# Where a matmul's two operands stand in a 128-byte row: weights of every sixth unit placed instead of one activation chunk, and modulation products emitted one unit later

## The chip, the cores and the metric

The kernel runs on one core of one Trainium2 chip. The metric is the device time of one launch in microseconds (us). Before the change the median of three runs is 2653.69 us (2653.15 to 2655.44).

## The reference

The reference is a two-layer encoder trunk on 256 tokens of 2048 features, all in float32. Cut to what matters:

```python
for l in range(DEPTH):                                   # 2 layers
    mod = silu(c) @ ada_w[l] + ada_b[l]                  # 6 * 2048 values
    sh_a, sc_a, gt_a, sh_m, sc_m, gt_m = split(mod, 6)
    h = rmsnorm(x, norm_mix[l]) * (1 + sc_a) + sh_a
    qa, ka, va, qb, kb, vb, ga, gb = split_cols(h @ w_in[l])
    ya = window_attention(qa, ka, va, sink) @ w_proj_a[l]
    yb = neighbourhood_attention(qb, kb, vb, bias) @ w_proj_b[l]
    x = x + gt_a * ((sigmoid(ga) * ya + sigmoid(gb) * yb) @ w_out[l])
    h = rmsnorm(x, norm_ffn[l]) * (1 + sc_m) + sh_m
    g, v = split(depthwise_conv(h @ w_up[l]), 2)         # 2 * 5632 channels, width 3 over tokens
    x = x + gt_m * ((silu(g) * v) @ w_down[l])
```

Nearly all of the arithmetic is products with the weight matrices. The change concerns the last three lines (the feed-forward) and the first two (the modulation `mod`).

## The kernel before

**Number format and matmuls.** Every operand of a matmul is split in two parts of the type fp32r: a high part, which is the value as ScalarE's cast writes it, and a low part, which is what the value has beyond it. A product takes three matmuls: high weights by high activation (L347), high weights by low activation (L348), low weights by high activation (L349). That is `feature_block`: one block of weights of 128x128 is stationary, and a chunk of activations of 128 features by 256 tokens moves. A chunk holds its high and low parts side by side, 256 values each. In another form, `tokens` (L410 to L412), the chunk of activations is stationary and 512 columns of weights move; it is used in the attention part.

**The stream of weights.** All weights of a layer are one list of 128x128 blocks in the order in which PE uses them, cut into 232 units of 16 blocks (1 MB each). `unit_steps` fetches a unit by one DMA (L319) into the pool `raw`, which has four buffers, and makes its two halves of eight blocks: ScalarE casts the high part (L330), VectorE subtracts it from the value for the low part (L331). The halves live in the pool `hl`, which has four buffers. A half must be read to its end by PE before its buffer is cast anew.

**The feed-forward.** It begins at unit 100 of each layer. A group of channels goes through w_up (16 blocks for a column of 128 channels, one for each of the 16 chunks of the normalised input `h`), then through w_down (one block for each channel chunk `act` of the group, for each of the 16 outputs). There are three groups, of 14, 17 and 13 chunks (FF_GROUPS), so a layer has 88 columns of w_up and 44 x 16 blocks of w_down. The first 12 columns of w_up run on "bare" chunks, which are not yet scaled by the norm and carry two more columns (258); the levelling comes behind them. From unit 112 on w_up runs on `h`.

**The place in a row of 128 bytes.** OFF is 48 floats and ROW is 64 floats. Two addresses are called at the same place here if they are equal modulo 32 floats, which is 128 bytes. `led` lays `h` out with chunk 0 at 0 and the others behind 48 further floats, so that chunk 0 stands 64 bytes off the other fifteen. The weights of the feed-forward stand at offset 0 in their buffer (`at = 0` in `unit_steps`). So fifteen chunks of sixteen differ from the weights by 64 bytes, and one, chunk 0, is at the same place. `chunks_of` does the like for the `act` chunks: the last chunk of a group is moved by 16 floats and is at the same place as the weights; the others are 64 bytes off. Such a chunk is called set apart in what follows, and a matmul whose successor's weights are at the same place as its own moving chunk is called a matching one.

**The modulation.** `mod` has 96 columns of 128 values in each layer. For each, a 1 MB tile of `ada_w` is fetched by a DMA (L236) into the same four buffers as the weights, and one VectorE instruction (L237) multiplies it with silu(c) and sums it, followed by a small one that reads the sum. `plan(l, u)` runs when PE's stream has used up a unit (`tick`), and issues as many columns as ADA_PLAN_0 and ADA_PLAN_1 ask for at this unit; `need(l, n)` runs them at once where a value is about to be used. The columns of layer 1 begin in layer 0's feed-forward, and the last are made in layer 1's.

**What sets the order.** The order of the instructions on each engine is found by the scheduler of the framework from the order of emission and its own estimate of times, except for the instructions that `keep_in_program_order` holds at their place. Units are emitted when the stream first asks for one (`next_block`), modulation columns at the tick before it.

## Time and profile before

| What | Value |
| --- | --- |
| median of 3 runs | 2653.69 us |
| the profiled execution | 2656.99 us |
| its span, first to last instruction | 2655.2 us |
| outside the span | 1.8 us |
| granted TensorE clock | 1.000 |
| PE busy | 2642.3 us |
| VectorE (DVE) busy | 2120.4 us |
| ScalarE (ACT) busy | 1408.2 us |
| GpSimd (POOL) busy | 227.7 us |
| moved from and to HBM | 700 MB, 264 GB/s |

A row of the timeline gives the start in the span, the duration, engine, line of the code, operation, tiles (`out<-in`) and shapes; a bracket at its end gives the idle time of the engine before it and what released it. PE's matmuls are pipelined: one starts long before its predecessor has ended, so the duration of 0.28 us is not what a matmul costs. What it costs is the step, the time from its start to the start of the next, and over a stretch without gaps the steps are counted and divided. PEld is the loading of a weight block into the array. It runs beside the matmul before it.

### The profile page before, as it was taken

The numbers are of one execution on the slowest core, as the hardware profiler recorded it, in microseconds if no ns is written. First come the engines' busy times: TensorE is split into PE (matmuls) and PEld (weight loads), VectorE is DVE, ScalarE is ACT, GpSimd is POOL, SyncE is SP. The second block draws the span as 40 slices with busy tenths as digits, with TensorE's granted clock in tenths as the row PEclk, the third lists the DMA queues.
The fourth block names the chain that finished last, engine by engine and source line by source line (L and its number), as shares of the span: only waits on it lengthen the run. The fifth ranks groups of instructions, "written<-read, shape, count | busy, mean of one in ns | idle before, by whom it ended". The sixth has DMA issues, their size and how long they took to land.

```text
span 2655.2 us, 51015 instructions
## 1 busy us (share of the span) xinstructions
PE 2642.3 (100%) x21164; PEld 2556.4 (96%) x21164; DVE 2120.4 (80%) x2979; ACT 1408.2 (53%) x2280; POOL 227.7 (9%) x345
## 2 busy tenths in 40 slices
PE   9999999999999999999999999999999999999999
PEld 7888899999999999999998889999999999999999
DVE  8898998897987888688886777868888866655664
ACT  5445865456653554355564666555565445544553
POOL 0001100000000000000002558620000000000000
PEclk9999999999999999999999999999999999999999
DMA  9988779885777877777756666667747765555554
GB/s 357 351 328 303 259 292 361 327 315 203 288 295 286 294 290 287 298 284 289 287 223 254 254 231 226 254 258 264 278 184 287 297 246 191 194 196 194 195 191 143
DMA packets 102186, 700.46 MB, mean 264 GB/s; under 512 B 12865, under 2 KB 15169, under 8 KB 18113
## 3 DMA queue, kind: packets, MB, share of 16 engines
q1 hardware_dynamic: 101954, 697.20, 71.0%
q8 instruction: 165, 2.70, 0.4%
q14 instruction: 67, 0.55, 0.1%
HBM read 695.06 MB, written 2.10 MB: 263 GB/s over the span
## 4 chain that ended last, share of the span: by engine, by line
PE 81%; DMA 8%; DVE 7%; issue 3%; ACT 1%; POOL 0%; DVEq 0%; ACTq 0%
PE ps L347 22%; PE ps L349 22%; PE ps L348 22%; DMA aw<-in_aw 8%; PE ps_t L411 4%; PE ps_t L412 4%; PE ps_t L410 4%; DVE hl L331 3%; DVE aw L237 2%; PE sc L655 1%; PE po L693 1%; ACT hl L330 1%; DVE u L1056 0%; PE warm L445 0%; PE cb L754 0%
## 5 line engine op out<-in xcount | busy, mean ns | idle before, releaser
L331 DVE TENSOR_TENSOR hl<-w,hl 128x1024 fp32r<-128x1024 f32 x928 | 1131.5, 1226 | 295.8 <-ACT hl L330 291.4
L330 ACT CAST hl<-w 128x1024 fp32r<-128x1024 f32 x928 | 970.0, 1049 | 707.3 <-PE ps L349 489.2
L347 PE MATMUL ps<-h,hl 128*128 128x256 f32 x3328 | 922.0, 277 | 1.3 <-DVE ya L977 0.6
L348 PE MATMUL ps<-h,hl 128*128 128x256 f32 x3328 | 919.2, 276 | 0.0
L349 PE MATMUL ps<-h,hl 128*128 128x256 f32 x3328 | 918.9, 276 | 0.0
L347 PEld LDWEIGHTS ps<-h,hl 128*128 128x128 f32 x3328 | 624.7, 188 | 2.4 <-DVE ya L977 0.8
L348 PEld LDWEIGHTS ps<-h,hl 128*128 128x128 f32 x3328 | 624.8, 188 | 0.4 <-DVE h L505 0.2
L349 PEld LDWEIGHTS ps<-h,hl 128*128 128x128 f32 x3328 | 624.3, 188 | 0.0
L237 DVE CUSTOM_DVE_ANT_0 aw<-aw,cact,ab 128x2048 f32<-128x2048 f32 x189 | 444.2, 2351 | 88.8 <-DMA aw<-in_aw 88.2
L411 PE MATMUL ps_t<-hl,h 128*128 128x512 f32 x576 | 225.1, 391 | 0.4
L410 PE MATMUL ps_t<-hl,h 128*128 128x512 f32 x576 | 223.2, 392 | 2.2 <-ACT h L504 1.6
L412 PE MATMUL ps_t<-hl,h 128*128 128x512 f32 x576 | 224.5, 391 | 0.0
L1056 DVE SCALAR_TENSOR_TENSOR u<-ps,cw,u 128x255 f32<-128x255 f32 x304 | 146.3, 481 | 62.4 <-ACT u L1054 58.4
L1054 ACT ACTIVATE u<-ps,cw 128x256 f32<-128x256 f32 x152 | 85.7, 564 | 149.2 <-PE ps L349 148.9
L349 PE MATMUL ps<-act_o,hl 128*128 128x256 f32 x512 | 141.5, 276 | 1.1 <-DVE hl L331 1.1
L349 PE MATMUL ps<-merged,hl 128*128 128x256 f32 x512 | 141.5, 277 | 0.0
L348 PE MATMUL ps<-act_o,hl 128*128 128x256 f32 x512 | 141.5, 276 | 0.0
L348 PE MATMUL ps<-merged,hl 128*128 128x256 f32 x512 | 141.5, 276 | 0.0
L347 PE MATMUL ps<-merged,hl 128*128 128x256 f32 x512 | 141.5, 277 | 0.0
L347 PE MATMUL ps<-act_o,hl 128*128 128x256 f32 x512 | 141.4, 277 | 0.0
L410 PEld LDWEIGHTS ps_t<-hl,h 128*128 128x128 f32 x576 | 107.9, 188 | 25.9 <-ACT h L504 2.7
L411 PEld LDWEIGHTS ps_t<-hl,h 128*128 128x128 f32 x576 | 108.1, 188 | 24.3 <-DVE hl L331 2.1
(244 smaller groups left out, 4805.1 us busy)
## 6 DMA issues: line engine op xcount, KB each, us to landing
w<-in_ws SPq DMA_DIRECT2D x463, 1024.0 KB, 4.9
aw<-in_aw SPq DMA_DIRECT2D x189, 1024.0 KB, 6.3
p<-in_bias SPq DMA_DIRECT2D x16, 256.0 KB, 5.0
x<-in_xT SPq DMA_DIRECT2D x4, 512.0 KB, 5.6
aw_o<-in_aw SPq DMA_DIRECT2D x2, 1024.0 KB, 12.5
out<-x SPq DMA_DIRECT2D x16, 128.0 KB, 2.1
w<-in_ws SPq DMA_DIRECT2D x2, 512.0 KB, 11.8
aw_b<-in_aw SPq DMA_DIRECT2D x1, 1024.0 KB, 18.0
```

The lines of the kernel that those rows point to most:

```text
L237: nc.vector.tensor_tensor_reduce(out=raw[:], in0=raw[:], in1=cact[:], scale=1.0, scalar=ab[:, i : i + 1], op0=ALU.mult, op1=ALU.add, accum ...
L330: nc.scalar.copy(hl[:, 0], r)
L331: nc.vector.tensor_tensor(out=hl[:, 1], in0=r, in1=hl[:, 0].bitcast(F32), op=ALU.subtract)
L347: nc.tensor.matmul(out, hi, act[0], start=first, stop=False)
L348: nc.tensor.matmul(ps[:, :S], hi, act[1], start=False, stop=False)
L349: nc.tensor.matmul(out, lo, act[0], start=False, stop=last)
L410: nc.tensor.matmul(ps[:], xh, hi, start=kc == kcs[0], stop=False)
L411: nc.tensor.matmul(ps[:], xh, lo, start=False, stop=False)
L412: nc.tensor.matmul(ps[:], xl, hi, start=False, stop=kc == kcs[-1])
L655: nc.tensor.matmul(sc[:, t], q[i][:, t * P : (t + 1) * P], k[j], start=i + j == 0, stop=(i, j) == by(q)[-1])
L1054: nc.scalar.activation(out=u, in_=ps, func=AF.Identity, scale=w[:, 1:2], bias=w[:, 3:4])
L1056: nc.vector.scalar_tensor_tensor(out=u[:, to], in0=ps[:, of], scalar=w[:, j : j + 1], in1=u[:, to], op0=ALU.mult, op1=ALU.add)
```

## The change

**Part one, the places.** In the feed-forward no chunk of `h` and no chunk of `act` is set apart any more: `led` puts chunk 0 of this `h` at 48 floats too, and `chunks_of` is told not to move the last chunk. Instead, from unit 113 on (`ff[l]`), every sixth unit of a layer (APART) has the first four blocks of its first half at an offset of 48 floats, at the same place as the moving chunks; its other four blocks stand at the usual place in the same buffer. For this half the cast and the subtraction write two pieces of 512 values instead of one of 1024 in each partition, and `feature_block` picks the piece. There are 20 such units in a layer, 113 to 227.

**Part two, the products.** A modulation product that `plan` asks for is no longer emitted at once if the unit is 108 or later, or if it is layer 1 and the unit is before 76 (HASTE is units 76 to 107, which stay as they were). Its DMA is issued as before, but the product goes to a list, `pending`, and is emitted when the stream has emitted the next unit (`use_landed` in `next_block`), or at the next `need`. These products are held in program order.

```diff
@@ chunks_of and led
-        at = [2 * S * k + (ROW - OFF if k == n - 1 and (k < room - 1 or tag in SPARE) else 0) for k in range(n)]
+        at = [2 * S * k + (ROW - OFF if apart and k == n - 1 and (k < room - 1 or tag in SPARE) else 0) for k in range(n)]
...
-    def led(name, apart=None):
+    def led(name, apart=None, lead=0):
...
-        at = [0] + [OFF + 2 * S * k for k in range(1, KC)]
+        at = [lead] + [OFF + 2 * S * k for k in range(1, KC)]
...
+    patient, pending = [False], deque()
+
+    def use_landed():
+        while pending:
+            pending.popleft()()
@@ ada
-            nc.vector.tensor_tensor_reduce(
...
+            def landed(raw=raw, i=i, held=True):
+                product = nc.vector.tensor_tensor_reduce(
...
+                if held:
+                    tc.keep_in_program_order(product)
...
+            if patient[0]:
+                pending.append(landed)
+            else:
+                landed(held=False)
@@ unit_steps
+        apart = u >= ff[l] and (u - ff[l]) % APART == 0
...
-            hl = hl[:, at : at + 2 * n].rearrange("p (a n) -> p a n", a=2)
+            if apart and j == 0:
+                hl = hl[:, 2 * (ROW - OFF) :].rearrange("p (g n) -> p g n", g=2)[:, :, ROW - OFF :]
+                hl = hl.rearrange("p g (a n) -> p a g n", a=2)
+                r = r.rearrange("p (g n) -> p g n", g=2)
+            else:
+                hl = hl[:, at : at + 2 * n].rearrange("p (a n) -> p a n", a=2)
@@ feature_block
+        if len(hl.shape) == 4:
+            hl, j = hl[:, :, j // 4], j % 4
@@ next_block, roots, plan, need, act_of
+                use_landed()
...
-            self.h = led(f"h{self.l}_{self.w}")
+            self.h = led(f"h{self.l}_{self.w}", lead=OFF * self.w)
...
+        patient[0] = u >= HASTE.stop or l > 0 and u < HASTE.start
...
+        patient[0] = False
...
+        use_landed()
...
-                    acts.extend(chunks_of(sp, tag, n // 2, f"act{l}_{gi}_{tag}", min(n // 2, len(chunks) - len(acts))))
+                    acts.extend(chunks_of(sp, tag, n // 2, f"act{l}_{gi}_{tag}", min(n // 2, len(chunks) - len(acts)), False))
```

**How the order moves.** In the rows below a tile's name is `hl`, layer, unit, half for the split weights, `aw`, layer, column for a tile of modulation weights, and `w`, layer, unit for the raw weights; L237 becomes L247, L331 becomes L356.

VectorE in layer 0's w_up on bare chunks, at unit 110, before:

```order
L237 ISA aw0_80_7438,mod0_172<-aw0_80_7438,cact_100,ab0_173 128x2048
L237 ISA mod0_172 128x1
L1056 SCALAR_TENSOR_TENSOR u_7363<-lev_7364,cw0_997,u_7363 128x255
L505 SCALAR_TENSOR_TENSOR h0_1_6804<-ht_7430,mod0_172,h0_1_6804 128x256
L1056 SCALAR_TENSOR_TENSOR u_7363<-lev_7364,cw0_997,u_7363 128x255
L505 SCALAR_TENSOR_TENSOR h0_1_6804<-ht_7434,mod0_172,h0_1_6804 128x256
L331 TENSOR_TENSOR hl0_110_0_7455<-w0_110_7453,hl0_110_0_7455 128x1024
L571 TENSOR_TENSOR lev_7441<-ps0_109_16_0_7373,rbs_6802 128x256
L331 TENSOR_TENSOR hl0_110_1_7458<-w0_110_7453,hl0_110_1_7458 128x1024
```

The same place after the change:

```order
L356 TENSOR_TENSOR hl0_110_0_7454<-w0_110_7452,hl0_110_0_7454 128x1024
L1087 SCALAR_TENSOR_TENSOR u_7363<-lev_7364,cw0_997,u_7363 128x255
L533 SCALAR_TENSOR_TENSOR h0_1_6804<-ht_7430,mod0_172,h0_1_6804 128x256
L1087 SCALAR_TENSOR_TENSOR u_7363<-lev_7364,cw0_997,u_7363 128x255
L533 SCALAR_TENSOR_TENSOR h0_1_6804<-ht_7434,mod0_172,h0_1_6804 128x256
L356 TENSOR_TENSOR hl0_110_1_7457<-w0_110_7452,hl0_110_1_7457 128x1024
L247 ISA aw0_80_7438,mod0_172<-aw0_80_7438,cact_100,ab0_173 128x2048
L247 ISA mod0_172 128x1
```

The product of column 80 stood ahead of both subtractions of unit 110, and now stands behind both; the first subtraction moved ahead of the four smaller instructions as well.

VectorE in layer 0's last w_down, where the three interleaved outputs are done and the residuals (L1029) and squares are made, at unit 228, before:

```order
L1029 SCALAR_TENSOR_TENSOR x_102<-ps0_226_8_0_14791,mod0_172,x_102 128x256
L458 TENSOR_TENSOR sqa_14338<-sqa_14338,sq_14843 128x256
L545 SCALAR_TENSOR_TENSOR bare1_0_b0_14341<-x_102,amod1_9459,bare1_0_b0_14341 128x256
L237 ISA aw1_45_15091,mod1_9454<-aw1_45_15091,cact_100,ab1_9455 128x2048
L237 ISA mod1_9454 128x1
L1029 SCALAR_TENSOR_TENSOR x_102<-ps0_227_5_0_14850,mod0_172,x_102 128x256
L331 TENSOR_TENSOR hl0_228_0_14963<-w0_228_14961,hl0_228_0_14963 128x1024
```

The same place after the change:

```order
L1060 SCALAR_TENSOR_TENSOR x_102<-ps0_226_8_0_14791,mod0_172,x_102 128x256
L356 TENSOR_TENSOR hl0_228_0_14962<-w0_228_14960,hl0_228_0_14962 128x1024
L486 TENSOR_TENSOR sqa_14338<-sqa_14338,sq_14843 128x256
L573 SCALAR_TENSOR_TENSOR bare1_0_b0_14341<-x_102,amod1_9459,bare1_0_b0_14341 128x256
L1060 SCALAR_TENSOR_TENSOR x_102<-ps0_227_5_0_14850,mod0_172,x_102 128x256
L356 TENSOR_TENSOR hl0_228_1_14965<-w0_228_14960,hl0_228_1_14965 128x1024
```

Column 45's product stood ahead of unit 228's first subtraction. Now no product stands in this piece: column 44's comes behind unit 228's second subtraction, and column 45's only behind unit 230's. At unit 222 it is the same: column 42's product stood between the two subtractions, and column 41's now stands behind both. PE's order of matmuls is the same save for the first two of unit 111, which stood among unit 110's and now stand behind them. On SyncE's queue the order of the large transfers is the same save for a few swaps, but a modulation tile holds its `raw` buffer until its later product has run.

More of the change, by code (lines that the diff above doesn't have):

```diff
@@ L61 @@
 ADA_PLAN_1 = [(8, 143), (76, 166), (84, 168), (99, 176), (108, 176), (128, 184), (142, 192)]
+HASTE = range(76, 108)
 FIRST_PLAN = [(0, 6), (10, 17), (42, 48)]
@@ L76 @@
 BARE = [8, 12]
+APART = 6
 SIDE = 4
@@ L236, in ada @@
             nc.sync.dma_start(raw[:], a["aw"][l, n])
[L237 to L247 removed]
+            def landed(raw=raw, i=i, held=True):
+                product = nc.vector.tensor_tensor_reduce(
+                    out=raw[:], in0=raw[:], in1=cact[:], scale=1.0, scalar=ab[:, i : i + 1],
+                    op0=ALU.mult, op1=ALU.add, accum_out=mod[:, i : i + 1],
+                )
+                if held:
+                    tc.keep_in_program_order(product)
+                part, kc = divmod(i, KC)
+                if part in (1, 4):
+                    w = part // 3
+                    nc.vector.scalar_tensor_tensor(
+                        out=amod[:, w, kc : kc + 1], in0=mod[:, i : i + 1], scalar=1.0, in1=nrm[:, w, kc : kc + 1],
+                        op0=ALU.add, op1=ALU.mult,
+                    )
+            if patient[0]:
+                pending.append(landed)
+            else:
+                landed(held=False)
             done[l] = n + 1
@@ L311, in turned_blocks @@
         moved_blocks(dst, blocks)
+    ff = [next(i for i, b in enumerate(seq) if b[0] == "w_up") // UB + BARE[1] * KC // UB + 1 for seq in STREAMS]
     def unit_steps(l, u, by_halves=False):
```

11 lines of the change are left out of this document (1 added, 10 removed).

## The prediction

> **What bounds the kernel now.** The first views are the page's head, the clock of the core, and the share of the chain that ended last.
>
> ```profile
> span 2655.2 us, 51015 instructions
> PE 2642.3 (100%) x21164; PEld 2556.4 (96%) x21164; DVE 2120.4 (80%) x2979; ACT 1408.2 (53%) x2280; POOL 227.7 (9%) x345
> ```
>
> ```profile
> core 0: 2655.2 us, clock 1.000
> ```
>
> PE is busy for all but 12.9 us of the span at the full granted clock, so the end moves only by what a matmul's step costs and by PE's gaps. VectorE is busy for 80% and can be late at a place without being the bound. The view of PE's waits from 680 us on shows what is left of gaps where the change acts:
>
> ```profile
> PE ps L349 <- DVE hl L331: 1.9, 2, 1.1
> PE sc L655 <- ACT packB L629: 0.7, 1, 0.7
> ```
>
> Two waits are for the low half of the weights. The third is for a packed score tile and has no product in it; it stays. So I go through the steps first and the gaps after.
>
> **Part one: the places.** A step is the time from one matmul's start to the next one's. In the rows below I count the matmuls between two starts by the program (three to a block) and divide.
>
> ```profile
> 1042.68 0.28 PE L347 MATMUL ps<-act_a,hl 128*128 128x256 f32 x1
> ...
> 1059.00 0.28 PE L347 MATMUL ps<-act_b,hl 128*128 128x256 f32 x1
> ```
>
> From the first matmul on group 1's act chunks up to just ahead of its set-apart chunk lie 48 blocks, 144 steps: 16.32 us, 113.33 ns each. No step there is matching. This is the base.
>
> ```profile
> 1004.46 0.28 PE L347 MATMUL ps<-h,hl 128*128 128x256 f32 x1
> ...
> 1037.22 0.28 PE L347 MATMUL ps<-h,hl 128*128 128x256 f32 x1
> ```
>
> These are six columns of w_up, 6 x 48 = 288 steps, in 32.76 us. At the base they would take 32.64. Each column has one set-apart chunk, three matching matmuls, so one such run of three costs 0.12 / 6 = 20 ns.
>
> A longer run, of twelve, stands where the attention output gives way to the merged branch:
>
> ```profile
> 533.81 0.28 PE L347 MATMUL ps<-oB,hl 128*128 128x256 f32 x1
> ...
> 535.70 0.28 PE L348 MATMUL ps<-merged,hl 128*128 128x256 f32 x1
> ```
>
> 16 steps in 1.89 us, against 16 x 113.33 = 1.813: 77 ns more, to the rounding of a row 80, which is four times 20. So the cost goes with the number of matching matmuls, at 6.7 ns each.
>
> That these runs come from the chunk here and from the weights after the change could matter. The stretch of w_in in the other form has rows that tell the two apart, since there only the stationary operand's place differs, for chunk 0:
>
> ```profile
> 1461.52 0.39 PE L410 MATMUL ps_t<-hl,h 128*128 128x512 f32 x1
> ...
> 1462.88 0.40 PE L410 MATMUL ps_t<-hl,h 128*128 128x512 f32 x1
> ...
> 1464.28 0.39 PE L410 MATMUL ps_t<-hl,h 128*128 128x512 f32 x1
> ```
>
> Six steps take 1.36 us, the next six, with the other place of the stationary chunk, 1.40. The moving tile's place is the same in both, so it is the relation between the two operands that costs. I take that a run costs the same whichever of the two was moved.
>
> Counting for a layer: w_up on h has 88 - 12 = 76 columns, and w_down three groups of 16 outputs, 48. Each had one set-apart chunk: 124 x 20 ns = 2.48 us. After the change there are 20 units with four matching blocks, twelve matmuls each: 20 x 80 ns = 1.60 us. The difference is 0.88 us a layer, **1.76 us** for both. Bounds: if a matching run cost nothing when it is made by the weights, 2 x 2.48 = 4.96 us go; if each of the 20 units cost twice as much, 160 ns, the sum is 2 x (2.48 - 3.20) = -1.44, a small loss. I take the middle, since the row with a run of twelve is the nearest.
>
> The cast and the subtraction of these 40 halves write two pieces of 512 instead of one of 1024. No row has this shape. Below nothing they cannot go, as the number of elements is the same; above, a second start of an instruction would be the most, and a subtraction as a whole takes 1.23 us (a row below). I take nothing. What hides it is the reserve between a half's cast and its first matmul:
>
> ```profile
> 728.90 1.05 ACT L330 CAST hl<-w 128x1024 fp32r<-128x1024 f32 x1 [1.24 <-PE ps L349]
> ...
> 736.88 0.28 PE L347 MATMUL ps<-h,hl 128*128 128x256 f32 x1
> ```
>
> From this cast's start to its half's first matmul are 7.98 us; without the cast's 1.05 and a subtraction's 1.23, 5.7 us are left. If that cover were gone, 40 halves at even 0.1 us each would be 4 us.
>
> **Part two: the products.**
>
> ```profile
> L237 DVE CUSTOM_DVE_ANT_0 aw<-aw,cact,ab 128x2048 f32<-128x2048 f32 x189 | 444.2, 2351 | 88.8 <-DMA aw<-in_aw 88.2
> ```
>
> A product takes 2.35 us, nearly two subtractions, and VectorE waits 88.2 us in all for the tiles to land, with everything behind it queued. Where that falls just ahead of a needed subtraction, PE waits. The rows around the first gap:
>
> ```profile
> 677.00 2.35 DVE L237 CUSTOM_DVE_ANT_0 aw<-aw,cact,ab 128x2048 f32<-128x2048 f32 x1
> ...
> 680.86 1.23 DVE L331 TENSOR_TENSOR hl<-w,hl 128x1024 fp32r<-128x1024 f32 x1
> ```
>
> ```profile
> 681.10 0.28 PE L348 MATMUL ps<-bare_a,hl 128*128 128x256 f32 x1
> 682.14 0.39 PE L349 MATMUL ps<-bare_a,hl 128*128 128x258 f32 x1 [0.77 <-DVE hl L331]
> 682.37 0.28 PE L347 MATMUL ps<-bare_a,hl 128*128 128x258 f32 x1
> ```
>
> The step from 681.10 lasts 1.04 us and the one behind it 0.23, two steps that should take 0.23 together (0.24 with the two extra columns): 1.03 us lost. The product is column 80's, and the order puts it behind both subtractions of unit 110 now, so the first of them runs 2.35 us sooner and more. The second gap, at unit 228 of layer 0:
>
> ```profile
> 1324.44 2.35 DVE L237 CUSTOM_DVE_ANT_0 aw<-aw,cact,ab 128x2048 f32<-128x2048 f32 x1 [1.61 <-DMA aw<-in_aw]
> ...
> 1327.12 1.22 DVE L331 TENSOR_TENSOR hl<-w,hl 128x1024 fp32r<-128x1024 f32 x1
> ```
>
> ```profile
> 1326.97 0.28 PE L348 MATMUL ps<-act_o,hl 128*128 128x256 f32 x1
> ...
> 1328.39 0.39 PE L349 MATMUL ps<-act_o,hl 128*128 128x256 f32 x1 [1.14 <-DVE hl L331]
> 1328.61 0.28 PE L347 MATMUL ps<-act_o,hl 128*128 128x256 f32 x1
> ```
>
> 1.42 + 0.22 instead of 0.23: 1.42 us lost (rows are rounded to 0.01). VectorE stood 1.61 us waiting for the tile and multiplied for 2.35. After the change this product is behind unit 230's subtractions. The third, at unit 222, is too short for the view of waits:
>
> ```profile
> 1291.37 2.35 DVE L237 CUSTOM_DVE_ANT_0 aw<-aw,cact,ab 128x2048 f32<-128x2048 f32 x1 [2.15 <-DMA aw<-in_aw]
> ...
> 1293.64 1.22 DVE L331 TENSOR_TENSOR hl<-w,hl 128x1024 fp32r<-128x1024 f32 x1
> ```
>
> ```profile
> 1295.07 0.28 PE L349 MATMUL ps<-act_y,hl 128*128 128x256 f32 x1
> 1295.31 0.39 PE L347 MATMUL ps<-act_o,hl 128*128 128x256 f32 x1
> 1295.54 0.29 PE L348 MATMUL ps<-act_o,hl 128*128 128x256 f32 x1
> ```
>
> 0.24 + 0.23 instead of 0.23: 0.25 us. Together 1.03 + 1.42 + 0.25 = **2.70 us**. What is late next at these places: the subtraction can start when its cast is done, and the reserve of 5.7 us is the bound on that; I take that nothing takes the gaps' place. The range of this term is 0 (the same waits somewhere else) to 2.70.
>
> What the wait of the product moved: a tile of modulation weights holds its `raw` buffer until its product has run, now about a unit later, some 5.4 us (48 steps of 113.33 ns). Behind it on SyncE's queue stand the next units' transfers.
>
> ```profile
> w<-in_ws SPq DMA_DIRECT2D x463, 1024.0 KB, 4.9
> aw<-in_aw SPq DMA_DIRECT2D x189, 1024.0 KB, 6.3
> ```
>
> A unit lands 4.9 us after its issue by the page's median. If a fetch is held up by a whole unit's time, 5.4 us, the reserve of 5.7 us just covers it. This is the thinnest cover in the change, and a rival is built on it.
>
> **Sum.** 1.76 + 2.70 = 4.46 us. The profiled execution of 2656.99 us becomes 2652.5. It lies 3.30 us above the median of 2653.69, and the same subtraction from the median gives **2649.2 us**, 0.17% less.
>
> **The rivals.**
>
> *The weights' place costs nothing.* If only a moving chunk's own change of place costs time, 4.96 goes in place of 1.76: 4.96 + 2.70 = 7.66, 2646.0 us. For it: nearly all runs of three in the trace have moved chunks, not moved weights. Against it: 1.36 and 1.40 us above, where the chunk that was moved is the stationary one.
> The Trainium skill ("TensorE: Matmul & The Clock Gate", "Step-by-step: what each phase is for") says that PE has two independent SBUF read ports and that loading the next weights takes no bandwidth from the running matmul. By that rule places would not matter at all, the first part would change nothing, and the sum would be the second part's. The trace speaks against it: 20 ns for each matching run.
>
> *The places do nothing together, or the products do nothing.* If the weights' runs cost what the chunks' did, the first part is nil: 2653.69 - 2.70 = 2651.0. If the gaps only move, because the later release of buffers holds up a unit's transfer or because other instructions fill the place ahead of a subtraction, the first part alone remains: 2653.69 - 1.76 = 2651.9. For it: the thin cover above, with 5.4 us against 5.7. With a few new gaps of 1 us as at 681 and 1327, five more than were removed, it would be 2657.
>
> *Slower: PE is left in a slower step.* The trace has a gait that is neither of the two, behind a run of four matching matmuls:
>
> ```profile
> 611.07 0.28 PE L347 MATMUL ps<-merged,hl 128*128 128x256 f32 x1
> ...
> 616.02 0.28 PE L347 MATMUL ps<-merged,hl 128*128 128x256 f32 x1
> ```
>
> 42 steps in 4.95 us, 117.9 ns each, with no matching step among them, until the next run brings back the base. Runs of three, six, nine and twelve leave the base as it was. Before the change a run came every 5.4 us and could set a wrong gait right at once; after it one comes every sixth unit, 33 us. If a run of twelve that the weights make, or the entry into h after the bare chunks, leaves PE in this gait, it stays there: 5760 matmuls of a layer (76 x 16 + 44 x 16 blocks, three each) at 4.6 ns are 26 us a layer, 53 us for both, so 2653.69 - 2.70 + 53 = 2704 at the worst, and 2677 if it holds half the time. The time is past the former one once 10% of the steps (4.46 / 53 and a little) are in it. Against it: twelve is a multiple of three, and the run of twelve above gave the base back.
>
> **How the numbers follow.** The forecast has 0.52, placement free 0.10, first part nil 0.05, products nil or gaps elsewhere 0.24, slow gait 0.09. A measurement of this kernel tells some 0.2%, 5.3 us, from no change: below 2648.4 is faster, above 2659.0 slower. The forecast stands 0.8 us above the first of these, so I give a third of it, 0.18, to faster, and 0.34 to the same; placement free is 0.10 of faster. Of the 0.29 without one of the parts 0.02 goes to faster and 0.03 to slower, where gaps come in number, the rest to the same. The slow gait is slower. That makes faster 0.30, same 0.58, slower 0.12. The range goes from 2645.5, just below the case of free placement, to 2655.5, above the case without products and with three or four new gaps of 1 us; what it leaves out is the slow gait and gaps in number.
>
> **What would show it.** In the trace of the changed kernel, 48 steps of a w_up column on h should take 5.44 us with no run of 20 ns in it, and the first twelve matmuls of units 113, 119 and so on 80 ns above the base. Steps of 118 ns between these units would mean the slow gait. PE should have no gap at the starts of units 110, 222 and 228. The median time from issue to landing of the modulation tiles, and waits of PE for the cast (L355) or the subtraction (L356), tell whether the later release costs. It is wrong if the first matmuls of those units cost nothing or much more than 80 ns, or if gaps as long stand elsewhere.

## The result

The changed kernel takes 2699.02 us (2698.77 to 2701.39, six runs), the kernel before beside it 2653.33 us. The ratio is 1.0169, with a 95% interval of 1.0159 to 1.0179: 45.7 us slower. The forecast was 2649.2 us. The time lies in the rival that had 0.09, PE left in a slower step.

The head of the profile after:

```profile
span 2697.0 us, 50997 instructions
PE 2685.5 (100%) x21164; PEld 2600.4 (96%) x21164; DVE 2123.2 (79%) x2979; ACT 1407.3 (52%) x2280; POOL 236.1 (9%) x345
```

PE has the same 21164 matmuls as before and is busy 43.2 us longer, VectorE 2.8. What a matmul costs has changed. The clock is no cause: the mean granted clock is 1.000 here as before. The view by windows counts the matmuls of a stretch in layer 0's feed-forward (length, PE busy and count, then the other engines, clock, DMA share, GB/s). Before:

```profile
900.00:1100.00 200.00, 200.00 (x1761) 200.00 (x1761) 166.23 (x210) 98.58 (x128) 0.00 (x0) 1.00 0.79 293
```

After:

```profile
900.00:1100.00 200.00, 200.00 (x1699) 200.00 (x1698) 160.48 (x207) 95.15 (x127) 0.00 (x0) 1.00 0.75 280
```

200 us / 1761 is 113.6 ns a matmul, 200 / 1699 is 117.7, with PE busy without a gap in both (two or three matmuls at the edges count too, so the quotient is a little low). VectorE, ScalarE and the transfers have less to do in the stretch after, as the units come slower. The timeline of PE shows where it begins, at the first unit with moved weights:

```profile
690.50 0.28 PE L374 MATMUL ps<-h,hl 128*128 128x256 f32 x1
...
695.15 0.28 PE L376 MATMUL ps<-h,hl 128*128 128x256 f32 x1
...
696.58 0.28 PE L376 MATMUL ps<-h,hl 128*128 128x256 f32 x1
...
729.09 0.28 PE L376 MATMUL ps<-h,hl 128*128 128x256 f32 x1
```

From 690.50 to 695.15 lie 41 steps of unit 112, 113.4 ns each. The matmul at 695.15 is the third of unit 112's last block, and the weights of unit 113's first block are loaded beside it:

```profile
695.15 0.19 PEld L374 LDWEIGHTS ps<-h,hl 128*128 128x128 f32 x1
```

So at 695.15 begins the run of twelve matching matmuls of unit 113, 1.43 us, 119.2 ns each or 70 ns above the base in all, forecast 80. From 696.58 to 729.09, where unit 119's run begins, lie 276 plain steps: 117.8 ns each. None matches, and none is at the base. It goes on so to the end of the feed-forward, in both layers: behind each run 276 steps with a mean of 117.8, and the further runs themselves at 120.0.

The gaps are gone. The only wait of PE behind 680 us in the view of waits is the one that was to stay:

```profile
PE sc L683 <- ACT packB L657: 0.7, 1, 0.7
```

And the group of the products shows VectorE waiting 5.7 us for tiles where it had waited 88.2; from issue to landing the tiles take 5.1 us by the median, where it was 6.3:

```profile
L247 DVE CUSTOM_DVE_ANT_0 aw<-aw,cact,ab 128x2048 f32<-128x2048 f32 x189 | 443.8, 2349 | 5.8 <-DMA aw<-in_aw 5.7
aw<-in_aw SPq DMA_DIRECT2D x189, 1024.0 KB, 5.1
```

To compare profiles without the start of the program, the table gives the time from the first matmul of unit 100 to the last of the layer, from the starts of the timeline's rows.

| Kernel | layer 0, us | layer 1, us |
| --- | --- | --- |
| before | 728.28 | 725.49 |
| before_again | 727.49 | 725.45 |
| the change | 749.05 | 748.91 |
| old_places (products alone) | 725.57 | 725.45 |
| old_products (places alone) | 750.08 | 748.92 |
| no_match | 723.14 | 723.02 |
| no_match_p1 | 724.16 | 723.01 |
| one_unit | 748.53 | 748.38 |
| lo_128 | 724.58 | 724.48 |
| lo_256 | 724.34 | 724.21 |

### The profile page after: what moved, and what is told of

Same layout as the page of the kernel before. It is cut to its first block, busy times and chain, and to the rows that moved or that the text cites. A ratio compares the mean times of both kernels' runs of the same rounds, so it can differ in the third digit from the quotient of the medians.

```text
span 2697.0 us, 50997 instructions
## 1 busy us (share of the span) xinstructions
PE 2685.5 (100%) x21164; PEld 2600.4 (96%) x21164; DVE 2123.2 (79%) x2979; ACT 1407.3 (52%) x2280; POOL 236.1 (9%) x345
## 4 chain that ended last, share of the span: by engine, by line
PE 93%; DVE 3%; ACT 2%; DMA 1%; issue 1%; POOL 0%; SPq 0%; ACTq 0%; DVEq 0%
PE ps L375 27%; PE ps L374 27%; PE ps L376 27%; PE ps_t L439 4%; PE ps_t L440 4%; PE ps_t L438 4%; DVE hl L356 1%; DVE aw L247 1%; ACT hl L355 1%; PE sc L683 1%; PE po L721 1%; DMA w<-in_ws 1%; ACT qsq L610 0%; POOL qrs L504 0%; DMA x<-in_xT 0%
## 5 line engine op out<-in xcount | busy, mean ns | idle before, releaser
L356 DVE TENSOR_TENSOR hl<-w,hl 128x1024 fp32r<-128x1024 f32 x928 | 1133.3, 1226 | 373.1 <-ACT hl L355 369.3
L374 PE MATMUL ps<-h,hl 128*128 128x256 f32 x3328 | 932.6, 280 | 1.3 <-DVE ya L1008 0.6
L375 PE MATMUL ps<-h,hl 128*128 128x256 f32 x3328 | 931.2, 280 | 0.0
L376 PE MATMUL ps<-h,hl 128*128 128x256 f32 x3328 | 930.7, 280 | 0.0
L247 DVE CUSTOM_DVE_ANT_0 aw<-aw,cact,ab 128x2048 f32<-128x2048 f32 x189 | 443.8, 2349 | 5.8 <-DMA aw<-in_aw 5.7
L375 PE MATMUL ps<-act_o,hl 128*128 128x256 f32 x512 | 143.9, 281 | 0.0
L376 PE MATMUL ps<-act_o,hl 128*128 128x256 f32 x512 | 143.9, 281 | 0.0
L374 PE MATMUL ps<-act_o,hl 128*128 128x256 f32 x512 | 143.6, 281 | 0.0
```

The source lines that it names most:

```text
L247: product = nc.vector.tensor_tensor_reduce(out=raw[:], in0=raw[:], in1=cact[:], scale=1.0, scalar=ab[:, i : i + 1], op0=ALU.mult, op1=ALU. ...
L356: nc.vector.tensor_tensor(out=hl[:, 1], in0=r, in1=hl[:, 0].bitcast(F32), op=ALU.subtract)
L374: nc.tensor.matmul(out, hi, act[0], start=first, stop=False)
L375: nc.tensor.matmul(ps[:, :S], hi, act[1], start=False, stop=False)
L376: nc.tensor.matmul(out, lo, act[0], start=False, stop=last)
```

## The experiments

The names of steps: the base is 113.3 ns, the slow step 117.8 ns. A matching matmul is one beside which the next matmul's weights, at the same place in 128 bytes as its moving chunk, are loaded.

### Which part costs: old_places and old_products

old_places undoes the places and keeps the later products:

```diff
-        apart = u >= ff[l] and (u - ff[l]) % APART == 0
+        apart = False
...
-            self.h = led(f"h{self.l}_{self.w}", lead=OFF * self.w)
+            self.h = led(f"h{self.l}_{self.w}", lead=0)
...
-                    acts.extend(chunks_of(..., False))
+                    acts.extend(chunks_of(...))
```

> The changed kernel with the places of before (chunk 0 of h and the last chunk of act set apart, no unit's weights moved) and the later products kept. Theory: all the loss is the slow step that begins at unit 113 with the first run of matching matmuls that the weights make. Then this kernel has 113.3 ns steps and 20 ns a column again, and the three gaps of 2.7 us are gone: about 2650.6 us. Rival 1, the later products cause the slow steps (by other timing of the weights at the entry to h): about 2699. Rival 2, the gaps come back at other places: 2653.

Measured: 2653.45 us against 2654.36, ratio 0.9997 (0.9987 to 1.0006). The stretch of layer 0 is 2.71 us shorter than in the profile of before, that of layer 1 the same; none of the three gaps is there. So rival 1 falls: the later products make nothing slow. The median is the 2653 of rival 2 and not the 2650.6 of the theory, but the profiled execution has no gap in another place. The interval of the medians reaches from 3.4 us less to 1.6 more, so they can't tell the two apart; before_again, below, says what the gaps were worth in four executions.

old_products keeps the places and emits the products as before:

```diff
-        patient[0] = u >= HASTE.stop or l > 0 and u < HASTE.start
+        patient[0] = False
```

> The changed kernel with the products emitted as before, the new places kept. Theory: slow steps of 117.8 ns from unit 113 of each layer on, and the gaps at 681, 1295 and 1327 us back, save that a slower PE waits less for VectorE: 2699 to 2701.7 us. Rival 1 (the products cause it): 2653.3 - 1.8 = 2651.5.

Measured: 2700.70 us, ratio 1.0176 (1.0162 to 1.0190). The window has the 1699 matmuls of the change. One gap came back:

```profile
PE ps L376 <- DVE hl L356: 0.8, 1, 0.8
```

It is the one at unit 110; the two late in layer 0 are absent here. The loss is wholly in the places.

### Does the base need the runs at all: no_match and no_match_p1

no_match leaves out the moved weights of every sixth unit, so nothing in the feed-forward matches from unit 112 on:

```diff
-        apart = u >= ff[l] and (u - ff[l]) % APART == 0
+        apart = False
```

> The changed kernel without the moved weights of every sixth unit: in the feed-forward no matching matmul is left from unit 112 on, and the products are later. Theory (the step turns slow only by a run that ends in the wrong way): the steps stay at 113.3 ns through the feed-forward, 2653.3 - 4.96 - 2.7 = 2645.7 us. Rival 3 (without a run of the chunk's kind now and then PE falls into the slow step by itself or at the first short wait, and it was those runs that held it at 113.3): slow for most of the feed-forward, 2670 to 2697 us.

Measured: 2648.03 us against 2654.36, ratio 0.9976 (0.9967 to 0.9986). This is the fastest of all kernels here. It gains 6.3 us where 7.66 was expected; the products, below, are the smaller part. The window:

```profile
900.00:1100.00 200.00, 200.00 (x1768) 200.00 (x1767) 166.16 (x212) 98.08 (x127) 0.00 (x0) 1.00 0.78 291
```

200 / 1768 is 113.1; all 5760 plain steps of the layer have a mean of 113.33. Rival 3 falls. The base holds over 650 us without any run, and the chunk's runs of the kernel before had held nothing that would have been lost. They only cost.

no_match_p1 is no_match with `patient[0] = False`.

> The kernel no_match (no matching matmul in the feed-forward) with the products emitted as before. Theory (places: 20 ns for each run that is gone, 248 runs): 4.96 us less than before. The later products then are worth the difference to no_match, 1.0 to 2.7 us. If this kernel is no faster than before, the plain step needs the runs after all, and no_match got its gain from the products.

Measured: 2654.76 us, ratio 1.0012 with an interval of 0.9990 to 1.0035. Its own twelve runs spread from 2649.50 to 2673.95, four of them above 2671, and those of before beside it from 2653.54 to 2664.30. No trace shows what made the long ones long. So the medians decide nothing here; I read the profile, of a run of 2650.05, instead. The stretch of layer 1, which no gap lengthens in any of these kernels, is 723.01 us against 725.45 in before_again: 2.44 us for 124 runs, 19.7 ns each. Layer 0 differs from no_match by 1.02 us, which is the gap at unit 110.

### Is one run enough: one_unit

```diff
-        apart = u >= ff[l] and (u - ff[l]) % APART == 0
+        apart = u >= ff[l] and u == ff[l]
```

> The changed kernel with weights moved in unit 113 of each layer alone (one run of twelve matching matmuls a layer, where the change has twenty; no other in the feed-forward). Theory 'lock': one such run leaves PE in the step of 117.8 ns and nothing in the plain steps behind it brings the base back, so the time is that of the changed kernel less 38 runs of about 12 x 2.2 ns, about 2698 to 2699 us. Rival 'wears off': PE returns to 113.3 ns by itself within some columns and it is the repetition every sixth unit that keeps it slow: about 2648 + 2 x 1.5 (a unit's worth or so) = 2648 to 2655 us.

Measured: 2699.71 us, ratio 1.0168 (1.0153 to 1.0183), the time of the change. The window, 200 us behind the only run:

```profile
900.00:1100.00 200.00, 200.00 (x1701) 200.00 (x1700) 161.42 (x208) 95.62 (x129) 0.00 (x0) 1.00 0.76 283
```

117.6 ns. So one run of twelve, 1.4 us long, sets the step of the 5700 matmuls behind it. The slow step doesn't wear off; PE is locked in it. The stretch is 0.52 us shorter than in the change, which is the other 19 runs: 19 x 12 x (120.0 - 117.8) = 0.50.

### Which runs lock: patterns and lengths

patterns moves chosen blocks of each unit of w_up, in twelve ways. To find room it lays the low parts 1056 floats behind the high ones (4224 bytes) and packs the moved blocks behind the rest.

```diff
+        his, los = PATTERNS[ups[l].index(u) % len(PATTERNS)]
...
+        for base, moved in ((0, his), (n * P + ROW // 2, los)):
+            rest = [b for b in blocks if b not in moved]
+            moved = [b for b in blocks if b in moved]
+            to = {b: base + P * i for i, b in enumerate(rest)}
+            to.update({b: base + P * (len(rest) + i) + OFF - ROW // 2 for i, b in enumerate(moved)})
```

> The kernel of before (chunk 0 of h set apart, so each column of w_up starts with a run of three that brings the base) in which the w_up units on h have weights moved by 16 floats in twelve patterns, one to a unit, in turn: none; low parts of blocks 4, 8, 12; high parts of these; both; both of 4 and 5; of 4 to 6; of 4 to 7; low of 4, 8, 12 with high of the blocks behind; both of a block and the high of the next; high of 5, 9, 13 with the low of two; high of 4 and 5; low of 4, 5, 6. Runs of 1 to 12 matching matmuls that begin at a block's last or second matmul. The casts and subtractions of these halves are cut into more pieces, so the whole time says nothing. Theory A (count): the step is at the base when the number of matching matmuls since the base is a multiple of three, except that the first of a run that begins behind an unmatching last matmul of a block costs nothing and isn't counted; so runs of 3, 6, 9, 12 by the weights leave 117.8 ns, single low parts leave it slow after the first and second and bring the base with the third. Theory B (the end): what counts is where in a block the run ends; runs that end at the third matmul bring the base, all runs of the weights end at the first or second and leave PE slow, three single ones too. Theory C (the length of twelve with the split half alone): short runs leave the base. By A and B the columns take 5.44 + up to 0.2 us; by C 5.44 plus 6.7 ns for each matching matmul.

Measured: none of the three. The whole time is 2671.01 us, but every kind of run came back to the base within some ten steps, save in unit 121, whose runs follow one another too closely to tell. Unit 118, with both parts of blocks 4 to 7, the run of twelve that locks in the change:

```profile
726.14 0.28 PE L398 MATMUL ps<-h,hl 128*128 128x256 f32 x1
...
728.27 0.28 PE L398 MATMUL ps<-h,hl 128*128 128x256 f32 x1
...
730.65 0.28 PE L398 MATMUL ps<-h,hl 128*128 128x256 f32 x1
```

The 18 steps from 726.14, which hold the run, take 2.13 us, 118.3 ns each. The 21 behind it to the next unit take 2.38, 113.3. Behind the chunk's own run at the column's start it takes some eleven steps to get back, where the kernel before takes two. So the kernel had changed something that matters. Two things differ from the change: the distance of the plain low parts, 4224 bytes in place of 4096, and where in the buffer the moved blocks stand. I took the first, and that gave lo_128. It also meant that the question had to be put again with the distances of the change, in lengths.

lengths moves blocks of the second half only, in the change's own layout (moved blocks first, at 48 floats, high then low parts; where only low parts are moved, all low parts stand ahead of the high ones). All distances between a block's parts are multiples of 512 bytes in the plain halves and where both parts are moved.

```diff
+    KINDS = [(0, 0), (0, 1), (0, 2), (0, 3), (1, 0), (2, 0), (1, 1), (2, 2), (3, 3), (4, 4), (8, 8)]
...
+        g = KINDS[ups[l].index(u) % len(KINDS)] if j else (0, 0)
```

> The kernel of before (chunk 0 of h set apart, a run of three by the chunk at every column's start) with weights of the second half of each w_up unit on h moved in the layout of the change (moved blocks first, at 48 floats, the rest behind at a multiple of 256 bytes), by eleven kinds in turn: none; low part of block 8; of 8 and 9; of 8 to 10; high part of 8; of 8 and 9; both parts of 8; of 8 and 9; of 8 to 10; of 8 to 11; of all eight. Theory 'lock by the weights': every kind that has a run made by the weights ends in steps of 117.8 ns to the column's end, and the next column's run by the chunk brings 113.3 back. Theory 'count': a single low part shifts by one, two by two, three by three, which is the base again; runs by both parts lose the first, so 3, 6, 9, 12 stay slow. Rival 'twelve alone': runs shorter than 12 leave the base.

Measured, over all 152 units of both layers: the six kinds from one low part to both parts of block 8 came in at the base in all 14 columns of each, and left PE slow to the end of the column in all 14. The smallest, one low part of one block, in unit 113:

```profile
698.19 0.28 PE L387 MATMUL ps<-h,hl 128*128 128x256 f32 x1
...
699.55 0.28 PE L387 MATMUL ps<-h,hl 128*128 128x256 f32 x1
...
699.77 0.28 PE L389 MATMUL ps<-h,hl 128*128 128x256 f32 x1
...
702.37 0.28 PE L387 MATMUL ps<-h,hl 128*128 128x256 f32 x1
```

12 steps in 1.36 us, 113.3, up to block 8; then one matching matmul, the one before 699.77; then 22 steps in 2.60 us, 118.2. One matching matmul is enough here, in a half whose high and low parts stand in another order; chunk_parts, below, has one with all weights in place. The counting theory falls, since three single low parts leave PE as slow as one. So does twelve alone. The four kinds with both parts of two to eight blocks came in slow, so they say nothing of the way in.

The second half of the expectation failed too: the chunk's run at the next column's start brings the base back behind the five kinds with one part moved, in all 14 columns of each. It doesn't behind any of the columns with both parts moved. PE came into unit 123, which has no moved weights, slow and left it slow:

```profile
753.02 0.28 PE L387 MATMUL ps<-h,hl 128*128 128x256 f32 x1
...
758.68 0.28 PE L387 MATMUL ps<-h,hl 128*128 128x256 f32 x1
```

48 steps in 5.66 us, 117.9 ns, with the chunk's run at their head. Yet the same run at the head of the next unit, 124, did bring the base back behind this slow column, as it did in all twelve such places. What a chunk's run needs to end the slow step stays open.

### Weights or the end of the run: chunk_parts

One part of chunk 10 of h is moved by 16 floats as well, in layer 0 the low part, in layer 1 the high one. No weights are moved.

```diff
+        if lone is not None:
+            for k in range(10, KC):
+                i = at[k] + (16 * lone if k == 10 else 32)
+                more = 16 if k == 10 else 0
+                chunks[k] = t[:, i : i + 2 * (S + more)].rearrange("p (a s) -> p a s", a=2)[:, :, :S]
```

> The kernel of before (chunk 0 of h set apart, three matching matmuls at each column's start) with one part of chunk 10 of h moved by 16 floats as well: in layer 0 its low part, which makes one matching matmul, a block's second; in layer 1 its high part, which makes a block's first and third match. All made by the chunk, none by the weights. Theory 'the end': what counts is that the last matching matmul is a block's third; so layer 0's columns run at 117.8 ns from chunk 10 on and layer 1's return to 113.3. Rival 'made by the weights': runs by a chunk leave the base whichever matmul they end at; then 113.3 behind chunk 10 in both layers. Rival 'two of three': an uneven count leaves PE slow, so both layers are slow behind chunk 10.

Measured: slow behind chunk 10 in all 76 columns of layer 0 and all 76 of layer 1, and at the base again ahead of chunk 10 in each. Layer 0's unit 113, from block 6, from the matching matmul of block 10, and the next column's start:

```profile
701.83 0.28 PE L353 MATMUL ps<-h,hl 128*128 128x256 f32 x1
...
703.31 0.28 PE L354 MATMUL ps<-h,hl 128*128 128x256 f32 x1
...
705.31 0.28 PE L353 MATMUL ps<-h,hl 128*128 128x256 f32 x1
```

13 steps in 1.48 us, 113.8; then 17 in 2.00, 117.6. Layer 1's unit 113, where the run ends at a block's third matmul:

```profile
2010.51 0.28 PE L353 MATMUL ps<-h,hl 128*128 128x256 f32 x1
...
2011.87 0.28 PE L353 MATMUL ps<-h,hl 128*128 128x256 f32 x1
2011.98 0.28 PE L354 MATMUL ps<-h,hl 128*128 128x256 f32 x1
2012.10 0.28 PE L355 MATMUL ps<-h,hl 128*128 128x256 f32 x1
2012.22 0.28 PE L353 MATMUL ps<-h,hl 128*128 128x256 f32 x1
...
2013.99 0.28 PE L353 MATMUL ps<-h,hl 128*128 128x256 f32 x1
```

12 steps in 1.36, 113.3; behind block 10's three, 15 steps in 1.77, 118.0. So it isn't the weights as such, since a chunk does it too, and not the end of the run. The third rival, an uneven count, is what both layers show here; against it stand the three single low parts and the three matching matmuls of both parts of block 8 in lengths, which left PE slow too. Put together with lengths: from the base, only a run that covers whole blocks, from a block's first matmul to a block's third, left PE at the base. A run made by whole blocks of weights can't do that, since the weights of a block's first matmul are loaded beside the third matmul of the block before: it begins one matmul early and ends one early.

### Which distance locks: lo_128 and lo_256

lo_128 is the change with the same moved blocks, but every low part from unit 113 on 1056 floats behind its high part. lo_256 has 1088 floats (4352 bytes) in the plain halves. The edit of lo_128:

```diff
+        his = los = range(4) if (u - ff[l]) % APART == 0 else ()
...
+        for base, moved in ((0, his), (n * P + ROW // 2, los)):
+            rest = [b for b in blocks if b not in moved]
```

> The changed kernel with the low part of every half from unit 113 on 128 bytes further from its high part (4224 bytes in place of 4096 or 2048), the moved blocks of every sixth unit as before at 64 bytes off the others. Modulo 128 bytes nothing differs, so if only the place in a row of 128 bytes counts, PE locks as in the changed kernel: about 2699 us. Theory 'more address bits': with the low parts 128 bytes off, a slow stretch ends by itself within some ten steps, as it did behind every run in the kernel with patterns, whose low parts stood so: no_match's 2648.0 + 40 runs of some 0.12 us = 2653 us.

Measured: 2651.90 us against 2654.37, ratio 0.9988 (0.9979 to 0.9998). The window:

```profile
900.00:1100.00 200.00, 200.00 (x1763) 200.00 (x1763) 166.45 (x216) 99.25 (x134) 0.00 (x0) 1.00 0.77 288
```

The same twenty runs of twelve a layer, and PE is at the base behind each within six steps. The stretch of a layer is 1.44 to 1.46 us longer than in no_match, 72 ns a run. The place in 128 bytes alone doesn't decide.

> The kernel lo_128 with the low parts of the plain halves 256 bytes further than in the changed kernel (4352 in place of 4096) where lo_128 had 128 (4224), and the moved blocks' distances multiples of 256 as well. lo_128 came back to 113.3 ns by itself. If it is the address bit of 128 bytes that broke the lock, this kernel locks: about 2699 us. If any distance other than 4096 breaks it, 2652 us.

Measured: 2651.10 us against 2657.01 in its round, ratio 0.9976 (0.9966 to 0.9986), 1764 matmuls in the window, 1.20 us a layer over no_match, 60 ns a run. It doesn't lock either. PE locked with 4096 bytes between the parts of the plain blocks, and with 3584 (both parts of block 8 in lengths), and came back with 4224 and 4352: of what was tried, the multiples of 512 lock.

That the distance decides isn't shown, though, and the address bit of 128 bytes isn't ruled out. Both kernels also put the moved blocks elsewhere: their high parts begin 2112 bytes into the buffer, which has the same size in all three, and in the change 192. That is the same place modulo 128 bytes, but 128 bytes apart modulo 256. In lo_128 the moved low parts stand as in the change modulo 256 and the plain low parts don't; in lo_256 it is the other way round. So a rule by the place modulo 256 bytes, with no distance in it, would fit these kernels as well. No run changes the distance alone.

### What a step costs by the distance of the operands: places

No chunk of h is set apart (all stand at 64 modulo 128 bytes), and each unit of w_up stands as a whole at another place.

```diff
+    PLACES = [(4 * (i // 2), i % 2 * 32) for i in range(16)]
...
+        s, more = PLACES[ups[l].index(u) % len(PLACES)]
...
+        at = [{b: base + P * i for i, b in enumerate(blocks)} for base in (s, s + n * P + more)]
```

> The kernel of before with no chunk of h set apart and the halves of a w_up unit on h at a place that goes by unit through 0, 16, 32 to 112 bytes, each once with the low part 4096 and once 4224 bytes behind the high one. It asks what a step costs by the distance of the two operands. If the row has two halves of 64 bytes and only these count: places 0, 16, 32, 48 give 113.3 ns and 64 to 112 give 120 ns (the chunks stand at 64 modulo 128), or a mixture for the places between; if bytes count one by one: 120 ns at 64 alone. If a lock needs the 4096 of distance: slow steps of 117.8 ns behind a matching unit only in the units with 4096.

Measured (mean of steps 25 to 45 of the first such unit, with 4096 and with 4224 bytes to the low part):

| Place of the weights, bytes | 0 | 16 | 32 | 48 | 64 | 80 | 96 | 112 |
| --- | --- | --- | --- | --- | --- | --- | --- | --- |
| 4096, ns | 113.33 | 118.81 | 117.29 | 120.00 | 118.62 | 120.00 | 119.90 | 118.10 |
| 4224, ns | 113.33 | 118.90 | 117.76 | 117.81 | 117.86 | 117.95 | 121.57 | 118.81 |

Each of the sixteen stands in eight or ten units; their steps differ by up to 1.7 ns at a place, and at 0 by nothing. The starts of units at 0 (two), at 16 and at 64 with the next one's:

```profile
858.49 0.28 PE L377 MATMUL ps<-h,hl 128*128 128x256 f32 x1
...
863.94 0.28 PE L377 MATMUL ps<-h,hl 128*128 128x256 f32 x1
...
869.39 0.28 PE L377 MATMUL ps<-h,hl 128*128 128x256 f32 x1
...
875.09 0.28 PE L377 MATMUL ps<-h,hl 128*128 128x256 f32 x1
...
903.50 0.29 PE L377 MATMUL ps<-h,hl 128*128 128x256 f32 x1
...
909.20 0.28 PE L377 MATMUL ps<-h,hl 128*128 128x256 f32 x1
```

A column takes 5.45 us at 0 and 5.70 at 16 and at 64. Both theories of halves and of single bytes fall: one distance of the eight, just 64 bytes, gives the base, and each other costs 4 to 8 ns a step. The units at 64 match in every matmul and take 118.6 and 117.9 ns, where the matching matmuls of the change take 120.0; their high parts stand 128 bytes from the change's moved ones modulo 256, one more sign that the place modulo 128 isn't all. Whether a lock needs the 4096 this kernel can't tell: behind each matching unit comes one that is slow by its own place.

### What the products were worth: before_again

The kernel of before, unchanged.

> The kernel of before, unchanged, for a second profile. The gap at unit 110 follows from the order alone (the product stands ahead of a subtraction that PE waits for), so it should be there again with 1.0 us. The gaps at units 222 and 228 had VectorE wait 2.15 and 1.61 us for a tile to land; if they go by when the tile lands, they can be absent or smaller, and the products' part of the forecast was then 1.0 us in most executions and not 2.7. If all three are there again, 2.7 us stands.

Measured: 2654.08 us. The gap at unit 110 is there with the same length, the one at unit 222 twice as long, the one at unit 228 nearly gone:

```profile
678.97 0.28 PE L349 MATMUL ps<-bare_a,hl 128*128 128x256 f32 x1
680.01 0.39 PE L350 MATMUL ps<-bare_a,hl 128*128 128x258 f32 x1 [0.76 <-DVE hl L332]
...
1293.07 0.28 PE L350 MATMUL ps<-act_y,hl 128*128 128x256 f32 x1
1293.60 0.39 PE L348 MATMUL ps<-act_o,hl 128*128 128x256 f32 x1 [0.25 <-DVE x L1030]
...
1325.52 0.33 PE L350 MATMUL ps<-act_o,hl 128*128 128x256 f32 x1
1325.69 0.28 PE L348 MATMUL ps<-act_o,hl 128*128 128x256 f32 x1
```

1.04 us, some 0.5, and 0.06. (The stretch of layer 0 is 1.92 us longer than in old_places; the other 0.3 is slow steps, not gaps.) With no_match_p1 and old_products, where the late two are absent, four executions with the old products had 2.7, 1.6, 1.0 and 1.0 us of gaps. The one at unit 110 follows from the order; the other two go by when a tile lands.

## Why the prediction was wrong, point by point

**The base and the price of a chunk's run: right.** 113.33 ns in no_match, and 2.44 us a layer for the 124 runs, forecast 2.48.

**What stands behind a run was put at nothing: this is the step that failed.** The sum had 20 x 80 ns = 1.60 us a layer for the runs made by weights, from "the cost goes with the number of matching matmuls". The runs themselves cost that, 70 ns the first and 80 each other. But the 276 plain steps behind each take 117.8 ns, and a layer's stretch is 25.9 us longer than in no_match (749.05 against 723.14) where 1.60 was forecast. "I take that a run costs the same whichever of the two was moved" looked at a difference that isn't the one: in chunk_parts a run made by the chunk leaves PE slow too. What differs is whether the run covers whole blocks. In the trace of before nearly every run does, from a first matmul to a third, because a moved chunk makes them so. I took the run at 533.81 as the nearest row because it has twelve; it began at a block's first matmul, and the runs of the change begin at a third. The row that was nearest in kind was the run of four at 611.07, which doesn't cover whole blocks and left PE slow. I had quoted it for the rival, and gave it no place in the sum.

**The rival of the slow gait: right in its mechanism, wrong in what was held against it.** "Twelve is a multiple of three" is no protection: runs of 1, 2, 3 and 12 matching matmuls all locked PE where they were out of step with the blocks. Its place was right (unit 113, the first run) and its extent (5700 steps a layer at 4.45 ns). Its worst price of 2704 left out that the chunk's runs are gone too: 2653.69 - 2.70 - 4.96 + 53 = 2699.0, and 2699.02 was measured. That they agree so closely is luck: the two stretches are 51.8 us longer than in no_match, not 53, and the products gave less than 2.70, which about makes up for it. With 0.09 it had too small a share, since a stretch of the trace showed that a lock exists and nothing in the trace showed a weights' run that ends well.

**The rival "places nothing together": wrong**, and so are the bounds of part one, -1.44 to 4.96. They hold what a run costs while it lasts. Had PE come back to the base, as in lo_128, the sum would have held: 2 x (2.48 - 1.44) = 2.08 us for part one, forecast 1.76.

The Trainium skill ("TensorE: Matmul & The Clock Gate", "Step-by-step: what each phase is for") says that loading the next weights takes no bandwidth from the running matmul. The runs don't agree: in places, where one unit differs from another only in where its weights stand, a step takes 113.33 ns at one of eight places and 117.3 to 120.0 at the other seven.

**The products: right in the place and sized by one execution.** All three gaps are gone, 2.71 us between the two profiles, forecast 2.70. But 1.7 of it went by when tiles landed in that execution. The four executions have 1.6 us in the mean. With that, no_match comes to 4.88 + 1.6 = 6.5 us, and 6.3 was measured; the 0.9 us of old_places in the medians has too wide an interval to tell 1.6 from 2.7.

**The thin cover: not needed.** No wait of PE came in place of the gaps, and VectorE's idle time for tiles fell from 88.2 to 5.7 us. The slower PE isn't the reason: in no_match, at the base, it is 8.3. A later product holds its buffer longer, but no longer blocks VectorE's queue.

**The entry into h after the bare chunks**, which the rival named as another way in, does no harm: 41 steps at 113.4 ns in unit 112.

What stays open is why the array behaves so. The runs show a state that holds over hundreds of microseconds, that plain steps keep, and that depends on addresses and on where in a block a run begins and ends; no run here shows what is in it, nor which of the addresses decides, the distance of the parts or the place modulo 256 bytes.

## What to carry to other kernels

A trace shows the cost of a pattern only in the phase in which it occurs there: before a pattern is made in another way, ask whether it begins and ends at the same instruction of the loop, and take the row that differs least in that, not in length. Where a trace shows a state that holds by itself, one event prices all the work behind it, so a small edit can cost far more than the edit's own instructions; a kernel with that single event (here one_unit) tells lock from repetition at once. And where a remedy is spread more thinly, try first whether it is needed at all: no_match, without any run, beat both kernels with 2648.03 us, ratio 0.9976.

## What the runs showed of the hardware

- A step of 256 columns in fp32r is 113.33 ns only where the next weights' place differs from the moving chunk's by 64 bytes modulo 128; the other seven distances in steps of 16 bytes cost 117.3 to 120.0 ns with the low part 4096 bytes behind the high one.
- The slow step of 117.8 ns holds at those 64 bytes too, once PE is in it. It lasted from one matching matmul to the end of the column in lengths, and over 650 us in one_unit.
- With 4224 or 4352 bytes between a block's high and low parts and the moved blocks at another place modulo 256 bytes, runs of twelve wore off within six steps, at 72 and 60 ns a run.
- A program's start varies: the first matmul of the weights' stream began at 21.2 us of the span in the profile of before, at 18.9 in that of the change, and between 18.7 and 21.6 in the others. The difference of the first two, 2.3 us, would be most of the 3.3 us by which the profiled execution of before stood above its median; no trace of an execution at the median shows it.
